# A hybrid encoder layer on one core: bias kept in DRAM in final form, and one DMA per tile for bias, q, k and v

## The chip, the core and the metric

The kernel runs on one core of a Trainium2 chip. The time is that of the device, in microseconds, the median of several executions. A core has five engines that matter here: TensorE (PE in the profile; its weight loads are listed apart as PEld), VectorE (DVE), ScalarE (ACT), GpSimd (POOL) and SyncE (SP), which issues all DMAs of this kernel. A DMA is carried out by up to 16 DMA engines, and SP issues its DMAs in a fixed order: when the next one has to wait for a tile, all that are behind it wait too.

## What is computed

One layer over 512 positions of width 2048, all in float32:

```
h = x @ w_in                                  # 512 x 8192: q, k, v, gate for group A and group B
ya = dilated attention, 16 heads of 64        # logits q.k / 8 + T5 bias by distance, masked to strides 1, 4, 16
yb = neighbourhood attention, 16 heads of 64  # 8 x 64 grid, window 8 x 16, learned bias by (row, column) distance
y = concat(ya * silu(gate_a), yb * silu(gate_b))
x = LayerNorm(2 ** 0.25 * x + y @ w_out)
```

Both attentions are done as dense softmaxes: the bias of a head holds, for 128 queries (8 grid rows x 16 columns) and all keys that can be reached, the bias minus a mask. The kernel subtracts a bias of the opposite sign and takes a minimum in place of a maximum.

## The kernel before

**Stages.** First the input projection in six blocks (`BLOCKS`: v of group A, v of group B, k A, q A, k B, q B), each of 1024 columns. `plain_block` does the first one directly and the others go through `strassen_block`, which does seven products of quarter size. Every float32 operand is split into a high and a low half (`split`, L82 on ScalarE and L83 on VectorE), and each product of tiles is three matmuls. Results are staged in two SBUF buffers (`vst`, tags t4 and t5) and stored to DRAM: v to `v_d[g]` (512 x 2048) by L187, k and q to `kq_d[kind, g]` (8 pairs x 128 x 2 x 512) by L202 and L205.

**Bias before attention.** After block 2 `prep_a` makes one row of 1024 biases per head of group A and writes it 16 times to `rows_d` (L142). After block 3 `prep_b` loads the learned biases of group B, subtracts them from a column mask (L158, L161) and writes 3 variants of 720 values per head and column to `gd` (L162), eight heads at a time. It uses one buffer for its source (tag b0) and one for its result `gt` (tag b1).

**Attention.** 32 heads in 16 pairs; four score tiles per head, so n runs from 0 to 127 (`scores(n)`, head n // 4). PE's order is written out by hand: the scores of tile n, the transposes of tile n - 3 (`turn`), the values of the head before (`values`), and between them `fill(...)`, which takes the next matmuls from a stream of other work: first the gates (16 `gate_unit`s, two weight tiles of 512 KB each), then the first half of the output projection (`out_first`, four column blocks of four weight tiles). What is issued on the other engines and on SP is ordered by the scheduler of the language, from its own estimate of times.

**Loads in attention.** `load_pair(i)` fills the tiles of pair i (tags t0 to t3 for even pairs, t4 to t7 for odd ones): two k tiles, one q tile, one v tile, of 128 x 1024 float32, 512 KB each. A k tile holds the same 64 rows twice, in partitions 0 to 63 and 64 to 127, by two DMAs (L411); q takes four DMAs of 64 partitions (L413), v four of 128 (L418). `load_bias(h)` fills one of two bias buffers (b0, b1) by eight DMAs of 16 partitions each: 560 values per partition out of `rows_d` for group A (L449), 3 x 384 out of `gd` for group B (L452). VectorE reads the bias in L430. Weight tiles for the gates and for `out_first` go through two raw buffers, `raw_ring` (r8, r9), by L110. `out_first` issues four loads of z (the residual x, L546) ahead of its weights.

After attention the second half of the output projection and the normalisation follow (L597 on). They are not touched.

Of the kernel before, what the change touches and what calls it, by code (L numbers as in the profile page):

```python
# [18 lines left out]
PADB = 16  # L19
RPBW = 16 * RPB + 2 * PADB  # L20
# [3 lines left out]
ROW = 1024  # L24
# [34 lines left out]
def _view(t, offset, dims):  # L59
    return bass.AP(tensor=t.tensor, offset=t.offset + offset, ap=dims)  # L60
# [5 lines left out]
def hybrid_layer(tc, xT, xn, w_in, w_gate, w_out, t5x, brow, rpb, cmask, eye, gain, lbias, out):  # L66
    nc = tc.nc
    from contextlib import ExitStack
    with ExitStack() as ctx:
# [3 lines left out]
        dram = ctx.enter_context(tc.tile_pool(name="dram", bufs=1, space=bass.MemoryType.DRAM))  # L73
# [4 lines left out]
        def f(ap):  # L78
            return ap.bitcast(F32)
# [9 lines left out]
        def slot(tag, dtype=F32, name=None):  # L89
            return arena.tile([128, sizes[tag[0]]], dtype, name=name or tag, tag=tag)  # L90
# [32 lines left out]
        nc.vector.memset(eps, EPS)  # L123

        rows_d = dram.tile([H, 16, ROW], F32, name="rows_d")
        gd = dram.tile([H * 16, 3, 720], F32, name="gd")
        kq_d = {(kind, g): dram.tile([PAIRS, 128, 2, S], F32, name=f"{kind}{g}_d") for kind in "kq" for g in range(2)}
        v_d = [dram.tile([S, D], F32, name=f"v{g}_d") for g in range(2)]

        def prep_a():  # L130
            nc.sync.dma_start(ident, eye)
            bt = ring_b.next("bias")
            t5 = bt[0:33, 1024:1040]
            nc.sync.dma_start(bt[0:33, :ROW], brow)
            nc.sync.dma_start(t5, t5x)
            row = ring_b.next("bias")
            for i in range(2):
                ps = bank(pss, "sc")
                nc.tensor.matmul(ps[0:16], t5, bt[0:33, 512 * i:512 * i + 512], start=True, stop=True)
                nc.scalar.activation(row[0:16, 512 * i:512 * i + 512], ps[0:16], AF.Copy)  # L140
            for c in range(16):
                nc.sync.dma_start(rows_d[:, c], row[0:16, :ROW])  # L142

        def prep_b():
            for g in range(2):
                b0 = slot("b0", F32, "rpbs")
                r = b0[:, :720].rearrange("p (d j) -> p d j", d=15)
                masks = b0[:, 720:864].rearrange("p (v j) -> p v j", v=3)
                nc.sync.dma_start(masks, cmask)
                for hh in range(8):  # L150
                    h = 8 * g + hh
                    nc.sync.dma_start(r[16 * hh:16 * hh + 16],
                                      _view(rpb, PADB + h * RPB - 1, [[RPBW - 1, 16], [31, 15], [1, 48]]))
                for v in range(3):
                    gt = slot("b1", F32, "gt")[:, :720].rearrange("p (d j) -> p d j", d=15)
                    w = 32 if v == 0 else 48
                    o = 16 if v == 0 else 0
                    nc.vector.tensor_tensor(gt[:, :, 0:w], masks[:, v:v + 1, 0:w].to_broadcast([128, 15, w]),  # L158
                                            r[:, :, o:o + w], ALU.subtract)
                    if w < 48:  # L160
                        nc.vector.tensor_copy(gt[:, :, w:], masks[:, v:v + 1, w:].to_broadcast([128, 15, 48 - w]))  # L161
                    nc.sync.dma_start(gd[128 * g:128 * g + 128, v], gt)  # L162


        X = [slot(f"x{k}", F32R, f"xk{k}").rearrange("p (s q) -> p s q", s=2) for k in range(KT)]
# [15 lines left out]
        def store_v(g, ch, T, src):  # L181

            o = vst.next("vst", F32R).rearrange("p (h e) -> p h e", h=8)
            s = src.rearrange("p (h e) -> p h e", h=8)
            nc.scalar.activation(o[:, :, 0:64], s, AF.Copy)
            nc.vector.tensor_tensor(o[:, :, 64:128], s, f(o[:, :, 0:64]), ALU.subtract)
            nc.sync.dma_start(v_d[g][128 * T:128 * T + 128, 1024 * ch:1024 * ch + 1024], f(o.rearrange("p h e -> p (h e)")))  # L187

        def store_kq(kind, g, ch, half, b, src):

# [179 lines left out]
        for i, (kind, g) in enumerate(BLOCKS[1:], 1):  # L370
            strassen_block(w_in[16 * i:16 * i + 16], kind, g)
            if i == 2:
                prep_a()
            if i == 3:
                prep_b()

        back = slot("s0", F32, "xback").rearrange("p (k q) -> p k q", k=8)
        for k in range(8):
# [4 lines left out]
        raw_ring, sg_ring = Ring("r8", "r9"), Ring(*(f"n{i}" for i in range(6, 12)))  # L383
# [17 lines left out]
        def load_pair(i):  # L401

            g, j = divmod(i, PAIRS)
            t0 = 4 * (i % 2)
            ks, qs = [], []
            qt = slot(f"t{t0 + 3}", F32R, "q").rearrange("p (a n) -> p a n", a=2)
            for a in range(2):
                kt = slot(f"t{t0 + a}", F32R, f"k{a}").rearrange("p (s n) -> p s n", s=2)
                rows = slice(64 * a, 64 * a + 64)
                for d in range(2):  # L410
                    nc.sync.dma_start(f(kt[64 * d:64 * d + 64]), kq_d["k", g][j][rows])  # L411
                for s in range(2):
                    nc.sync.dma_start(f(qt[64 * s:64 * s + 64, a]), kq_d["q", g][j][rows, s])  # L413
                ks.append(kt)
                qs.append(qt[:, a].rearrange("p (b n) -> p b n", b=4))
            vv = slot(f"t{t0 + 2}", F32R, "vv").rearrange("p (b e) -> p b e", b=4)
            for b in range(4):
                nc.sync.dma_start(f(vv[:, b]), _view(v_d[g], 16 * b * D + 256 * j, [[64 * D, 8], [D, 16], [1, 256]]))  # L418
            return qs, ks, vv.rearrange("p b (h e) -> p b h e", h=2)

        def softmax(sc, bias, n, grp, by_act):
# [22 lines left out]
        def load_bias(h):  # L444
            bias = ring_b.next("bias")
            hg = h % 16
            for r in range(8):
                if h < 16:
                    nc.sync.dma_start(bias[16 * r:16 * r + 16, :560],  # L449
                                      _view(rows_d, hg * 16 * ROW + 463 - 64 * r, [[ROW - 1, 16], [1, 560]]))  # L450
                else:
                    nc.sync.dma_start(bias[16 * r:16 * r + 16].rearrange("p (v n) -> p v n", v=3),  # L452
                                      gd[16 * hg:16 * hg + 16, :, 48 * (7 - r):48 * (7 - r) + 384])
            biases[h] = bias

        def scores(n):
# [82 lines left out]
        def out_first(dc):  # L539

            if dc % 2 == 0:
                for t in range(4):
                    z[t].append(slot(f"x{6 + 2 * t + dc // 2}", F32, f"z{t}").rearrange("p (s q) -> p s q", s=2))
            accs = [bank(pacc, "acc") for _ in range(4)]
            for t in range(4):
                nc.sync.dma_start(z[t][dc // 2][:, dc % 2], xn[t * 128:t * 128 + 128, dc * 512:dc * 512 + 512])  # L546
            for u in range(4):
                wh, wl = out_load(raw_ring, dc, u)
                for t in range(4):
                    yield from out_mms(accs[t], t, u, wh, wl, u == 0, u == 3)  # L550
            for t in range(4):
                zt = z[t][dc // 2][:, dc % 2]
                nc.vector.scalar_tensor_tensor(zt, zt, ALPHA, accs[t], op0=ALU.mult, op1=ALU.add)

        def fillers():
            for _ in range(16):
                yield from gate_unit()
            z.extend([] for _ in range(4))
            for dc in range(4):
                yield from out_first(dc)  # L560
# [77 lines left out]
        for dc in range(2):  # L638
# [4 lines left out]
            for u in range(4, 8):  # L643
                wh, wl = out_load(out_ring, dc, u)
# [81 lines left out]
```

## Time and profile before

| | us |
|---|---|
| median of 3 runs | 1018.22 (1016.59 to 1019.3) |
| the profiled execution | 1024.81 |
| its span, from first to last instruction | 1022.7 |
| TensorE busy in it | 993.1 |
| VectorE busy in it | 752.7 |

The profile is that of one execution, 6.6 us above the median; its span leaves out 2.1 us around it. An engine's busy time counts its instructions; TensorE's matmuls are pipelined, so a busy TensorE is not one at its peak. "DMA share" is the mean busy share of the 16 DMA engines, from the records of their packets; a packet is put down to the stretch in which it starts, so a full stretch can show a little over 1. In the table of stretches each row has the length of the stretch, the busy time and the number of instructions of PE, PEld, DVE, ACT and POOL, the granted clock of TensorE, the DMA share and the GB/s. In the chain of waits each row has start, length and what ran or was waited for. In the timeline and in the list of issues "SPq" is SP's queue; a row's second number is the time that SP took to issue.

### The profile page before, as it was taken

What the parts mean: (1) busy time and instruction counts of PE and PEld (TensorE: products, weight loads), DVE (VectorE), ACT (ScalarE), POOL (GpSimd) and SP (SyncE); (2) the same over time, 40 slices, a digit from 0 to 9 for tenths busy, and PEclk for the clock granted to TensorE, in tenths of its full rate; (3) what the DMA queues carried; (4) which work ended last, traced back from release to release, by engine and by line L of the source; (5) the groups of instructions that cost most, each with busy time, mean ns of one, the idle gap of its engine ahead of it and who ended that gap; (6) DMA issues with size and microseconds to landing.
All of it is one profiled execution on the core that took longest, in us unless ns stands there. A gap on an engine that the chain in (4) does not pass through costs nothing.

```text
span 1022.7 us, 15990 instructions
## 1 busy us (share of the span) xinstructions
PE 993.1 (97%) x5901; PEld 875.0 (86%) x5901; DVE 752.7 (74%) x1257; ACT 517.8 (51%) x862; POOL 13.3 (1%) x13
## 2 busy tenths in 40 slices
PE   9999999999999999999999999999999788999995
PEld 6888888999999999999878888888888677888884
DVE  7826988887887977978577777777766555666677
ACT  6524445444444434445377777777666444656300
POOL 0000000000000000000000000000000000000022
PEclk9999999999999999999999999999999899999998
DMA  9933357347769438347965565566688886745212
GB/s 336 313 99 124 124 156 242 98 135 246 156 195 255 116 115 277 115 125 189 224 186 146 167 167 146 167 167 157 194 224 191 252 206 181 202 144 185 64 62 103
DMA packets 114645, 177.77 MB, mean 174 GB/s; under 512 B 49383, under 2 KB 73575, under 8 KB 114568
## 3 DMA queue, kind: packets, MB, share of 16 engines
q1 hardware_dynamic: 114568, 176.76, 59.1%
q8 instruction: 46, 0.75, 0.3%
q14 instruction: 31, 0.25, 0.1%
HBM read 144.09 MB, written 32.62 MB: 173 GB/s over the span
## 4 chain that ended last, share of the span: by engine, by line
PE 87%; DMA 5%; DVE 4%; SPq 2%; issue 1%; ACT 1%; ACTq 0%; DVEq 0%
PE acc L393 16%; PE acc L535 13%; PE acc L322 9%; PE acc L320 9%; PE acc L321 9%; PE pv L504 4%; PE pt L484 4%; PE acc L315 2%; PE acc L314 2%; PE acc L313 2%; DMA z<-in_xn 2%; PE acc L226 1%; PE acc L225 1%; PE sc L464 1%; PE sc L463 1%; PE acc L224 1%
## 5 line engine op out<-in xcount | busy, mean ns | idle before, releaser
L82 ACT ACTIVATE wh<-braw 128x1024 fp32r<-128x1024 f32 x140 | 148.1, 1060 | 191.4 <-PE acc L321 141.6
L83 DVE TENSOR_TENSOR wl<-braw,wh 128x1024 fp32r<-128x1024 f32 x140 | 170.6, 1222 | 51.1 <-ACT wh L82 50.9
L320 PE MATMUL acc<-xk,wh 128*128 128x256 f32 x512 | 143.3, 282 | 0.6 <-ACT wh L82 0.6
L321 PE MATMUL acc<-xk,wh 128*128 128x256 f32 x512 | 143.1, 281 | 0.0
L393 PE MATMUL acc<-xk,wh 128*128 128x512 f32 x512 | 142.6, 402 | 0.0
L322 PE MATMUL acc<-xk,wl 128*128 128x256 f32 x512 | 140.6, 281 | 0.0
L83 DVE TENSOR_TENSOR wl<-wraw,wh 128x1024 fp32r<-128x1024 f32 (+1 forms) x73 | 88.1, 1207 | 61.8 <-ACT wh L82 57.1
L82 ACT ACTIVATE wh<-wraw 128x1024 fp32r<-128x1024 f32 (+1 forms) x73 | 76.2, 1045 | 72.4 <-DMA wraw<-in_w_out 19.3
L432 ACT ACTIVATE p<-s,mn 128x512 f32<-128x512 f32 (+2 forms) x128 | 81.9, 640 | 60.6 <-DVE mn L430 59.4
L535 PE MATMUL acc<-wh,yk 128*128 128x512 f32 x320 | 108.6, 408 | 0.0
L320 PE MATMUL acc<-op,wh 128*128 128x256 f32 x384 | 107.2, 281 | 0.0
L321 PE MATMUL acc<-op,wh 128*128 128x256 f32 x384 | 107.2, 281 | 0.0
L322 PE MATMUL acc<-op,wl 128*128 128x256 f32 x384 | 105.1, 282 | 1.0 <-DVE wl L83 1.0
L393 PEld LDWEIGHTS acc<-xk,wh 128*128 128x128 f32 x512 | 91.2, 188 | 15.5
L320 PEld LDWEIGHTS acc<-xk,wh 128*128 128x128 f32 x512 | 97.3, 190 | 1.7 <-ACT bias L140 0.9
L321 PEld LDWEIGHTS acc<-xk,wh 128*128 128x128 f32 x512 | 97.3, 190 | 0.0
L327 DVE TENSOR_TENSOR braw<-braw 128x1024 f32<-128x1024 f32 x80 | 96.7, 1220 | 0.7
L322 PEld LDWEIGHTS acc<-xk,wl 128*128 128x128 f32 x512 | 95.8, 190 | 0.0
L490 ACT ACTIVATE th<-pt 128x512 fp32r<-128x512 f32 (+2 forms) x128 | 65.4, 511 | 41.4 <-PE pt L484 40.2
L491 DVE TENSOR_TENSOR tl<-pt,th 128x512 fp32r<-128x512 f32 (+2 forms) x128 | 75.0, 586 | 15.3 <-ACT th L490 14.1
L484 PE MATMUL pt<-ident,p 128*128 128x128 f32 x416 | 67.3, 276 | 13.7 <-DVE tl L491 10.5
L484 PEld LDWEIGHTS pt<-ident,p 128*128 128x128 f32 x416 | 53.2, 142 | 30.5 <-issue 9.8
(157 smaller groups left out, 1866.5 us busy)
## 6 DMA issues: line engine op xcount, KB each, us to landing
braw<-in_w_in SPq DMA_DIRECT2D x80, 512.0 KB
wraw<-in_w_gate SPq DMA_DIRECT2D x32, 512.0 KB
k<-k_d SPq DMA_DIRECT2D x64, 256.0 KB
wraw<-in_w_out SPq DMA_DIRECT2D x32, 512.0 KB
bias<-gd SPq DMA_DIRECT2D x128, 72.0 KB
v_d<-vst SPq DMA_DIRECT2D x16, 512.0 KB
k_d<-kst SPq DMA_DIRECT2D x32, 256.0 KB
q_d<-kst SPq DMA_DIRECT2D x64, 128.0 KB
```

What stands on the lines that cost most here:

```text
L82: nc.scalar.activation(hi, raw, AF.Copy)
L83: nc.vector.tensor_tensor(lo, raw, f(hi), ALU.subtract)
L320: nc.tensor.matmul(o, h[:, c], ah, start=k == 0 and n == 0, stop=False)
L321: nc.tensor.matmul(o, h[:, c], al, start=False, stop=False)
L322: nc.tensor.matmul(o, l[:, c], ah, start=False, stop=k == 7 and n == 1)
L327: nc.vector.tensor_tensor(dst[u], dst[u], other[u], ALU.add)
L393: nc.tensor.matmul(acc, w[:, k * 128:k * 128 + 128], X[8 * u + k][:, s], start=u == 0 and n == 0 and k == 0, stop=u == 1 and n == 2 and k ...
L432: nc.scalar.activation(p[:, :n].rearrange("p (b r c) -> p b r c", r=8, c=16), s[:, :n].rearrange(order, r=8, c=16), AF.Exp, bias=mn, scale ...
L484: nc.tensor.transpose(pt[:, k], p[:, k * 128:k * 128 + 128], ident)
L490: nc.scalar.activation(th, pt[:, :nch], AF.Copy)
L491: nc.vector.tensor_tensor(tl, pt[:, :nch], f(th), ALU.subtract)
L535: nc.tensor.matmul(acc, yk[k][:, s, c], w[:, wk], start=first and kk == 0 and n == 0, stop=last and kk == 1 and n == 2)
```

## The change

The bias of every head is written to DRAM in the form in which attention reads it, `bias_d`: 16 heads x 128 x 560 for group A, 16 x 128 x 1152 for group B. `prep_a` builds its part from `rows_d` by eight DMAs from DRAM to DRAM. `prep_b` is called once for each half of the heads, after blocks 3 and 4, and stores each variant by eight DMAs. `load_bias` is then one DMA. `store_v` splits each tile's store in two, so that `v_d` has its rows in the order in which attention wants them, and v is loaded by one DMA; k takes one DMA per tile, whose source is read twice by a step of 0; q takes two DMAs. `out_first` takes its weights through four buffers (r8, r9, x14, x15) and issues each z load behind a weight load.

```diff
@@ hybrid_layer
-        gd = dram.tile([H * 16, 3, 720], F32, name="gd")
+        bias_d = dram.tile([H, 128, 560], F32, name="biasa_d"), dram.tile([H, 128, 1152], F32, name="biasb_d")
@@ prep_a
+            for r in range(8):
+                nc.sync.dma_start(bias_d[0][:, 16 * r:16 * r + 16],
+                                  _view(rows_d, 463 - 64 * r, [[16 * ROW, 16], [ROW - 1, 16], [1, 560]]))
@@ prep_b
-        def prep_b():
-            for g in range(2):
...
+        def prep_b(g):
...
-                    nc.sync.dma_start(gd[128 * g:128 * g + 128, v], gt)
+                gt = gt.rearrange("p d j -> p (d j)")
+                for k in range(8):
+                    nc.sync.dma_start(bias_d[1][8 * g:8 * g + 8, 16 * k:16 * k + 16, 384 * v:384 * v + 384],
+                                      gt[:, 48 * (7 - k):48 * (7 - k) + 384])
@@ store_v
-            nc.sync.dma_start(v_d[g][128 * T:128 * T + 128, 1024 * ch:1024 * ch + 1024], f(o.rearrange("p h e -> p (h e)")))
+            o = o.rearrange("p h e -> p (h e)")
+            for r in range(2):
+                nc.sync.dma_start(_view(v_d[g], 16 * (2 * T + r) * D + 1024 * ch, [[128 * D, 4], [D, 16], [1, 1024]]),
+                                  f(o[64 * r:64 * r + 64]))
@@ hybrid_layer
-            if i == 3:
-                prep_b()
+            elif i in (3, 4):
+                prep_b(i - 3)
@@ load_pair
-            for a in range(2):
-                kt = slot(f"t{t0 + a}", F32R, f"k{a}").rearrange("p (s n) -> p s n", s=2)
-                rows = slice(64 * a, 64 * a + 64)
-                for d in range(2):
-                    nc.sync.dma_start(f(kt[64 * d:64 * d + 64]), kq_d["k", g][j][rows])
-                for s in range(2):
-                    nc.sync.dma_start(f(qt[64 * s:64 * s + 64, a]), kq_d["q", g][j][rows, s])
...
+            at = 128 * 2 * S * j
+            for s in range(2):
+                nc.sync.dma_start(f(qt[64 * s:64 * s + 64]),
+                                  _view(kq_d["q", g], at + S * s, [[2 * S, 64], [128 * S, 2], [1, S]]))
...
+            for a in range(2):
+                kt = slot(f"t{t0 + a}", F32R, f"k{a}")
+                nc.sync.dma_start(f(kt), _view(kq_d["k", g], at + 128 * S * a, [[0, 2], [2 * S, 64], [1, 2 * S]]))
...
-            for b in range(4):
-                nc.sync.dma_start(f(vv[:, b]), _view(v_d[g], 16 * b * D + 256 * j, [[64 * D, 8], [D, 16], [1, 256]]))
+            nc.sync.dma_start(f(vv), _view(v_d[g], 256 * j, [[D, 128], [128 * D, 4], [1, 256]]))
@@ load_bias
-            for r in range(8):
-                if h < 16:
-                    nc.sync.dma_start(bias[16 * r:16 * r + 16, :560],
-                                      _view(rows_d, hg * 16 * ROW + 463 - 64 * r, [[ROW - 1, 16], [1, 560]]))
-                else:
-                    nc.sync.dma_start(bias[16 * r:16 * r + 16].rearrange("p (v n) -> p v n", v=3),
-                                      gd[16 * hg:16 * hg + 16, :, 48 * (7 - r):48 * (7 - r) + 384])
+            n = 560 if h < 16 else 1152
+            nc.sync.dma_start(bias[:, :n], bias_d[h // 16][hg])
@@ out_first
-            for t in range(4):
-                nc.sync.dma_start(z[t][dc // 2][:, dc % 2], xn[t * 128:t * 128 + 128, dc * 512:dc * 512 + 512])
             for u in range(4):
-                wh, wl = out_load(raw_ring, dc, u)
+                wh, wl = out_load(first_ring, dc, u)
+                nc.sync.dma_start(z[u][dc // 2][:, dc % 2], xn[u * 128:u * 128 + 128, dc * 512:dc * 512 + 512])
                 for t in range(4):
                     yield from out_mms(accs[t], t, u, wh, wl, u == 0, u == 3)
...
+        first_ring = Ring("r8", "r9", "x14", "x15")
```

In a view such as `[[0, 2], [2 * S, 64], [1, 2 * S]]` each pair is a step and a count, in elements, the outermost first.

More of the change, by code (lines that the diff above doesn't have):

```diff
@@ L142, in prep_a @@
                 nc.sync.dma_start(rows_d[:, c], row[0:16, :ROW])
-        def prep_b():
-            for g in range(2):
[L146 to L161, printed above, removed]
-                    nc.sync.dma_start(gd[128 * g:128 * g + 128, v], gt)
@@ new lines, in prep_a @@
+            for r in range(8):
+                nc.sync.dma_start(bias_d[0][:, 16 * r:16 * r + 16],
+                                  _view(rows_d, 463 - 64 * r, [[16 * ROW, 16], [ROW - 1, 16], [1, 560]]))
+        def prep_b(g):
+            b0 = slot("b0", F32, "rpbs")
+            r = b0[:, :720].rearrange("p (d j) -> p d j", d=15)
+            masks = b0[:, 720:864].rearrange("p (v j) -> p v j", v=3)
+            nc.sync.dma_start(masks, cmask)
+            for hh in range(8):
+                h = 8 * g + hh
+                nc.sync.dma_start(r[16 * hh:16 * hh + 16],
+                                  _view(rpb, PADB + h * RPB - 1, [[RPBW - 1, 16], [31, 15], [1, 48]]))
+            for v in range(3):
+                gt = slot("b1", F32, "gt")[:, :720].rearrange("p (d j) -> p d j", d=15)
+                w = 32 if v == 0 else 48
+                o = 16 if v == 0 else 0
+                nc.vector.tensor_tensor(gt[:, :, 0:w], masks[:, v:v + 1, 0:w].to_broadcast([128, 15, w]),
+                                        r[:, :, o:o + w], ALU.subtract)
+                if w < 48:
+                    nc.vector.tensor_copy(gt[:, :, w:], masks[:, v:v + 1, w:].to_broadcast([128, 15, 48 - w]))
+                gt = gt.rearrange("p d j -> p (d j)")
+                for k in range(8):
+                    nc.sync.dma_start(bias_d[1][8 * g:8 * g + 8, 16 * k:16 * k + 16, 384 * v:384 * v + 384],
+                                      gt[:, 48 * (7 - k):48 * (7 - k) + 384])
@@ L404, in load_pair @@
             t0 = 4 * (i % 2)
-            ks, qs = [], []
             qt = slot(f"t{t0 + 3}", F32R, "q").rearrange("p (a n) -> p a n", a=2)
-            for a in range(2):
-                kt = slot(f"t{t0 + a}", F32R, f"k{a}").rearrange("p (s n) -> p s n", s=2)
-                rows = slice(64 * a, 64 * a + 64)
-                for d in range(2):
-                    nc.sync.dma_start(f(kt[64 * d:64 * d + 64]), kq_d["k", g][j][rows])
-                for s in range(2):
-                    nc.sync.dma_start(f(qt[64 * s:64 * s + 64, a]), kq_d["q", g][j][rows, s])
-                ks.append(kt)
-                qs.append(qt[:, a].rearrange("p (b n) -> p b n", b=4))
+            at = 128 * 2 * S * j
+            for s in range(2):
+                nc.sync.dma_start(f(qt[64 * s:64 * s + 64]),
+                                  _view(kq_d["q", g], at + S * s, [[2 * S, 64], [128 * S, 2], [1, S]]))
+            qs = [qt[:, a].rearrange("p (b n) -> p b n", b=4) for a in range(2)]
+            ks = []
+            for a in range(2):
+                kt = slot(f"t{t0 + a}", F32R, f"k{a}")
+                nc.sync.dma_start(f(kt), _view(kq_d["k", g], at + 128 * S * a, [[0, 2], [2 * S, 64], [1, 2 * S]]))
+                ks.append(kt.rearrange("p (s n) -> p s n", s=2))
             vv = slot(f"t{t0 + 2}", F32R, "vv").rearrange("p (b e) -> p b e", b=4)
-            for b in range(4):
-                nc.sync.dma_start(f(vv[:, b]), _view(v_d[g], 16 * b * D + 256 * j, [[64 * D, 8], [D, 16], [1, 256]]))
+            nc.sync.dma_start(f(vv), _view(v_d[g], 256 * j, [[D, 128], [128 * D, 4], [1, 256]]))
             return qs, ks, vv.rearrange("p b (h e) -> p b h e", h=2)
```

## The prediction

> **What bounds the kernel now.** I read the page's first two parts, then the table of stretches, then the chain of waits, then the DMA queue inside the stage that the change touches.
>
> ```profile
> PE 993.1 (97%) x5901; PEld 875.0 (86%) x5901; DVE 752.7 (74%) x1257; ACT 517.8 (51%) x862; POOL 13.3 (1%) x13
> q1 hardware_dynamic: 114568, 176.76, 59.1%
> ```
>
> TensorE is busy 993.1 of 1022.7 us, so all the waits together are worth under 30 us; DMA has two fifths of its time free on average. The table of stretches says where (length, then busy us of PE, PEld, DVE, ACT, POOL, then granted clock, DMA share of the 16 engines, GB/s):
>
> ```profile
> 250.00:330.00 80.00, 79.26 (x661) 77.40 (x660) 65.67 (x71) 34.60 (x39) 0.00 (x0) 1.00 0.73 188
> 330.00:410.00 80.00, 79.71 (x662) 79.31 (x662) 65.80 (x68) 35.33 (x39) 0.00 (x0) 1.00 0.57 176
> 489.00:910.00 421.00, 407.71 (x2060) 340.37 (x2059) 286.00 (x680) 263.42 (x532) 0.00 (x0) 0.98 0.69 185
> 790.00:814.00 24.00, 18.47 (x90) 15.45 (x88) 11.19 (x29) 9.55 (x22) 0.00 (x0) 0.86 0.84 234
> 838.00:862.00 24.00, 19.59 (x84) 16.18 (x85) 13.80 (x38) 10.54 (x24) 0.00 (x0) 0.86 0.72 178
> ```
>
> In attention (489 to 910 us) PE idles 421.00 - 407.71 = 13.3 us, most of it between 790 and 862. The chain of waits names who is late there:
>
> ```profile
> 765.38 5.29 DMA bias<-gd
> 773.28 6.26 DMA z<-in_xn
> 779.56 8.73 DMA z<-in_xn
> 797.52 5.57 DMA z<-in_xn
> 829.89 7.69 DMA k<-k_d
> 840.82 6.05 DMA wraw<-in_w_out
> ```
>
> These are loads queued behind one another. So the kernel is bound by TensorE, with one crowded patch of DMA; the change can win at most those 13.3 us and, at a clock of 0.86 in two stretches of 24 us, about 2 x 24 x 0.14 = 7 us more. It can lose far more if its "large" DMAs turn out to take longer.
>
> **The change part by part. First, the k loads.** Before, each 512 KB k tile is filled by two DMAs of 64 rows of 4 KB. After, it is one DMA whose source is walked as 2 copies (step 0) x 64 rows x 1024 elements. What outermost count does to a DMA can be read from the v load, whose source is walked as 8 x 16 x 256:
>
> ```profile
> 499.97 2.48 SPq L418 DMA_DIRECT2D vv<-v_d  x4
> 502.50 2.40 SPq L411 DMA_DIRECT2D k<-k_d  x4
> 87.10:88.20 1.10, 1.10 (x6) 0.90 (x6) 1.10 (x2) 0.00 (x0) 0.00 (x0) 1.00 0.89 361
> 502.00:504.00 2.00, 2.00 (x10) 1.65 (x10) 0.00 (x0) 0.00 (x0) 0.00 (x0) 1.00 0.48 158
> 506.50:511.00 4.50, 4.50 (x22) 3.72 (x21) 2.67 (x8) 1.53 (x4) 0.00 (x0) 1.00 1.03 229
> 700.10:701.10 1.00, 1.00 (x6) 0.76 (x5) 1.00 (x5) 0.66 (x2) 0.00 (x0) 1.00 0.60 154
> ```
>
> All four v issues are out by 502.45 and k issues follow at once, yet from 502 to 504 the DMA share is 0.48: the v packets keep half of the engines busy and the other half has none. k (outermost count 64, behind them from 506.5) fills all 16 (1.03), and so does the v store (128 partitions, 0.89 with its ends cut off). I read: a DMA is dealt to as many engines as its outermost counts allow, 8 for the v load, and **2 for the new k load**. The trace of before has no DMA with a count of 2, so this step is an inference, and it decides the sign.
>
> The Trainium skill says the same ("DMA: Bandwidth & Descriptors", section "Why a DMA increments its semaphore by 16 and not by 1"): a DMA uses the largest number of engines up to 16 that divides the slowest count of both access patterns. By that rule the v load gets 8, with which 0.48 agrees; no run here yet shows a count of 2.
>
> Price of one engine: the v store moves 361 / (0.89 x 16) = 25.4 GB/s per engine, 0.161 us for a 4 KB row. The new k DMA has 128 rows, 64 per engine: 64 x 0.161 = 10.3 us. 16 pairs x 2 tiles x 10.3 = **330 us on two engines**. Now, 32 tiles of 524 KB (16.8 MB) at 229 / 1.03 = 222 GB/s are 75 us of every engine.
>
> What else those two engines carry in attention: 0.69 x 421 = 290 us, less 75 for k, is 215. The bias loads go from 16 partitions to 128 at a time:
>
> ```profile
> k<-k_d SPq DMA_DIRECT2D x64, 256.0 KB
> bias<-gd SPq DMA_DIRECT2D x128, 72.0 KB
> vv<-v_d SPq DMA_DIRECT2D x64, 128.0 KB
> bias<-rows_d SPq DMA_DIRECT2D x128, 35.0 KB
> ```
>
> 128 x 72 KB + 128 x 35 KB = 14.0 MB, at 154 / 0.60 = 257 GB/s of all engines (the stretch at 700 us, bias alone) is 55 us; at 16 x 25.4 = 406 GB/s it would be 35. So 215 - 20 = 195. v keeps its bytes, on 16 engines instead of 8: twice the engines for half the time, nothing on the sum. q keeps 64 partitions per DMA: nothing.
>
> Sum on the two engines: 330 + 195 = 525 us, where the stage has 421. Free time of an engine now is 0.31 x 421 = 131 us, the k loads add 255: this can't be hidden. **Attention gets 525 - 421 = 104 us longer** if the two engines never idle. They will idle a little, since SP issues in a fixed order and waits at its head for tiles that a stalled PE gives free late; I take 3% of 525, 16 us. Bounds: if k is dealt to 16 engines, 16.8 MB at 406 GB/s is 41 us, 34 less than now; if every wait for bias adds on top (third rival), 90 us more.
>
> **Who waits, and for whom.** All DMAs stand in one queue per engine, so a load dealt to 16 engines lands when the two loaded engines get to it. k is issued early enough for one such delay, bias hardly:
>
> ```profile
> 577.43 3.75 SPq L449 DMA_DIRECT2D bias<-rows_d  x8
> 581.22 1.09 SPq L411 DMA_DIRECT2D k<-k_d  x2
> 588.98 1.08 SPq L411 DMA_DIRECT2D k<-k_d  x2
> 594.27 4.30 SPq L449 DMA_DIRECT2D bias<-rows_d  x6
> 593.78 0.69 DVE L430 CUSTOM_DVE_ANT_0 s<-sc,bias 128x512 f32<-128x512 f32 x1
> ```
>
> The bias issued from 577.43 is first read at 593.78, a lead of 16.3 us; the next one stands behind two k tiles (20.6 us). VectorE would wait in L430, with the low halves of the weights (L83) and of the probabilities (L491) behind it on its queue, and TensorE for those.
>
> **Bias laid out in DRAM (prep_a, prep_b).** New: 8 DRAM-to-DRAM DMAs of 16 heads x 16 rows x 2240 B (4.6 MB, outermost 16: all engines), and 48 stores of 197 KB (9.4 MB) for 6 of 360 KB (2.2 MB). The stores' target is walked as 8 heads x 16 rows: 8 engines by the reading above, 16 rows each; at 25.4 GB/s per engine 9.4 MB take 46 us, 23 per group. The first: nearest row 257 GB/s, 18 us for one pass, twice that if reading and writing add. The free share from 250 to 330 is 0.27 x 80 = 22 us, against 18 + 23 less 5 for the stores removed = 36; from 330 to 410 it is 34 us for 23. About 14 us too much in the first block; the weight tiles' lead covers a part. Also each `gt` waits until eight stores have read its only buffer, 8 us instead of about 1, and on VectorE the weights' low halves stand behind it. I take **+10 us**, between -1 (all hidden) and +30 (every excess and each of the four waits in full). The extra SP time (48 + 8 - 6 issues) is hidden: SP isn't on the chain before 765.
>
> **v stores.** Each tile's store becomes two of 64 partitions, outermost count 4:
>
> ```profile
> 85.98 22.63 SPq L187 DMA_DIRECT2D v_d<-vst  x8
> ```
>
> Now the eight stores of the first block are issued over 22.6 us, 2.8 apart. On 4 engines each takes 16 x 0.161 = 2.6 us, 5.2 per tile; two staging buffers give no more. The fourth to sixth tiles hold accumulator banks that the second product needs. The sixth is late by about 5 x (5.2 - 2.8) = 12 us, against some 8 us until its bank is wanted: **+4 us**, between 0 and +12. The second v block's stores lie far apart: nothing.
>
> **Output projection's first half.** Four raw buffers instead of two, and z loads one at a time between weights. That takes away the three z waits of the chain and 6.05 us of weights, if the queue is free; x14 and x15 come free only when the last gate has read X. In my forecast the two loaded engines are late there anyway: nothing. Fewer issues (28 to 7 per pair, 0.3 to 0.6 us each) are worth only the SPq steps in that patch: nothing, same reason.
>
> **Sum.** 104 + 16 + 10 + 4 = +134 us. The profiled execution took 1024.81 us (span 1022.7 and 2.1 around it); the median of the runs is 1018.22, 6.6 below. 1018 + 134 = 1152; I say 1150.
>
> **Rivals.**
> - *The k load is dealt to 16 engines after all* (split by its 128 partitions). Then attention's DMA falls by 34 for k and 20 for bias, from 0.69 to 0.56, and the queue between 765 and 862 goes: -13 for the idle time, up to -7 for the clock, +4 to +10 for the preparation: 1002 to 1015. For it: nothing but that the v load's half share has one example. It decides at 1018: faster if k has over about 8 engines (41 to 82 us of them). The Trainium skill has advice on this side too ("DMA: Bandwidth & Descriptors", section "Rules for kernel authors": coalesce small transfers; one 128-partition transfer rather than two halves), but the same table warns that an outermost zero-stride broadcast of c copies confines a DMA to c engines. No run here shows either yet.
> - *Two engines, but partly hidden.* k tiles lead by 1.5 pairs, and q and weights may be cheaper on uncrowded engines (215 falls to 160): 330 + 140 - 421 = +49, with 10 for the rest: 1060 to 1085.
> - *The bias waits come on top.* Both k tiles of a pair (20.6 us, some 24 with q and weights) stand ahead of a bias whose lead is 16.3 us: 8 us a pair, and half that again where PE then frees k tiles late and the two engines idle: 15 pairs x 6 to 8 = 90 to 120 more: 1230 to 1260.
> - *The change doesn't touch the bound*: waits of both signs cancel, 1015 to 1021. Only with k on about 8 engines.
>
> **Chances.** Forecast (1085 to 1215) 0.65; partly hidden 0.09; bias on top 0.13; 16 engines 0.10; no change 0.03. Faster by over 0.3% 0.10, within 0.3% 0.03, slower 0.87 (0.3% is about what a measurement of this kernel can tell from no change). The range that leaves out the last two cases and the end of the third: 1060 to 1245.
>
> **What would show it.** Right: stretches in attention with a DMA share near 0.13 at some 50 GB/s, PE idle for over 80 us between 489 and 1030, the chain led by k and bias loads; half shares during `prep_b`'s stores, quarter shares at 86 to 125. Wrong: k loads at a share near 1 and shorter attention. The largest doubt is the step from count 8 to count 2.

## The result, and the profile after

The median went from 1017.89 us (four runs now; the table above has the first three) to 1186.62 us: a ratio of 1.1653 with a 95% interval of 1.1623 to 1.1683, 168.7 us where 132 were forecast. The profiled execution took 1186.8 us, its span is 1185.0. The page after, its first parts and the shares of the chain, and behind them the shares of the chain before:

```profile
PE 1043.0 (88%) x5901; PEld 903.5 (76%) x5901; DVE 751.5 (63%) x1257; ACT 514.7 (43%) x862; POOL 13.3 (1%) x13
q1 hardware_dynamic: 112872, 188.55, 51.9%
PE 46%; DMA 39%; DVE 6%; SPq 3%; ACT 3%; issue 2%; DVEq 0%; POOL 0%; ACTq 0%; POOLq 0%
```

```profile
PE 87%; DMA 5%; DVE 4%; SPq 2%; issue 1%; ACT 1%; ACTq 0%; DVEq 0%
```

The engines do the same work (VectorE 751.5 us against 752.7), the DMA engines are on average less busy than before (51.9% against 59.1%), and yet DMA is now 39% of the chain that sets the end, where it was 5%. A mean over 16 engines hides what two of them do. The stages say where the time is. Here and below a block's stretch begins with its first matmul and ends with its last one or with the next block's first, and attention goes from the first gate matmul to the last score tile; first the five stretches after, then the same five before:

```profile
92.90:197.10 104.20, 84.83 (x337) 66.17 (x336) 66.14 (x68) 37.72 (x44) 0.00 (x0) 0.92 0.39 134
197.30:282.80 85.50, 83.08 (x678) 81.05 (x676) 69.76 (x72) 36.83 (x41) 0.00 (x0) 1.00 0.48 164
282.80:375.80 93.00, 84.64 (x673) 83.82 (x673) 64.92 (x68) 34.41 (x38) 0.00 (x0) 0.94 0.80 223
375.80:464.20 88.40, 83.08 (x674) 82.67 (x674) 68.05 (x71) 35.03 (x38) 0.00 (x0) 0.96 0.77 240
544.10:1096.80 552.70, 460.30 (x2138) 374.41 (x2137) 299.72 (x718) 273.10 (x558) 0.00 (x0) 0.91 0.50 147
```

```profile
93.90:169.90 76.00, 76.00 (x337) 62.92 (x337) 65.98 (x68) 36.45 (x41) 0.00 (x0) 1.00 0.54 180
170.10:252.60 82.50, 82.50 (x677) 80.88 (x675) 67.67 (x70) 37.01 (x41) 0.00 (x0) 1.00 0.46 154
252.60:332.80 80.20, 79.46 (x674) 79.22 (x674) 65.58 (x70) 34.16 (x38) 0.00 (x0) 1.00 0.76 199
332.80:414.20 81.40, 81.11 (x674) 80.70 (x673) 67.42 (x69) 35.06 (x38) 0.00 (x0) 1.00 0.56 174
494.10:934.50 440.40, 427.11 (x2140) 355.94 (x2138) 301.50 (x718) 275.97 (x558) 0.00 (x0) 0.98 0.67 183
```

The rows are the block v B, the blocks k A, q A and k B, and attention. They grew by 28.2, 3.0, 12.8, 7.0 and 112.3 us, together 163.3; the span grew by 162.3, so the rest is as long as before. TensorE's 460.30 busy us in attention against 427.11 are the same matmuls at a granted clock of 0.91 for 0.98 (427.11 x 0.98 / 0.91 = 460). In these rows the clock is lowest where TensorE idles most: 0.92 with 19 of 104 us idle in the block v B, 0.91 with 92 of 553 in attention, 1.00 with none.

Two stretches of the table of the changed kernel in which little but one kind of DMA runs, and what the chain waits for in the block v B and in attention:

```profile
88.60:99.60 11.00, 7.16 (x32) 5.60 (x30) 0.69 (x1) 0.60 (x1) 0.00 (x0) 0.94 0.26 93
593.00:595.00 2.00, 0.13 (x1) 0.13 (x2) 2.00 (x3) 1.82 (x4) 0.00 (x0) 1.00 0.13 53
```

```profile
88.42 11.47 DMA v_d<-vst
101.90 8.95 DMA v_d<-vst
112.82 9.40 DMA v_d<-vst
...
166.98 11.65 DMA v_d<-vst
180.67 11.67 DMA v_d<-vst
194.38 12.91 DMA v_d<-vst
...
587.87 18.04 DMA bias<-biasa_d
615.35 19.82 DMA bias<-biasa_d
635.18 17.95 DMA wraw<-in_w_gate
...
897.61 25.04 DMA k<-k_d
```

The v stores, whose target has an outermost count of 4, run at a share of 0.26, a quarter of the engines. The k loads run at 0.13, two of sixteen, at 53 GB/s, 26.5 per engine. That is the step that the forecast had to infer. What the chain then names is mostly not k (2% of it): it is bias (16%) and weights (10%), which by the same reading are dealt to all engines and wait 18 to 20 us until the two loaded ones reach them. Whoever reads the names alone would blame the bias.

### The profile page after: what moved, and what is told of

Same layout as the page of the kernel before. It is cut to its first block, busy times and chain, and to the rows that moved or that the text cites. A ratio compares the mean times of both kernels' runs of the same rounds, so it can differ in the third digit from the quotient of the medians.

```text
span 1185.0 us, 15632 instructions
## 1 busy us (share of the span) xinstructions
PE 1043.0 (88%) x5901; PEld 903.5 (76%) x5901; DVE 751.5 (63%) x1257; ACT 514.7 (43%) x862; POOL 13.3 (1%) x13
## 3 DMA queue, kind: packets, MB, share of 16 engines
q1 hardware_dynamic: 112872, 188.55, 51.9%
## 4 chain that ended last, share of the span: by engine, by line
PE 46%; DMA 39%; DVE 6%; SPq 3%; ACT 3%; issue 2%; DVEq 0%; POOL 0%; ACTq 0%; POOLq 0%
DMA bias<-biasb_d 10%; PE acc L537 8%; DMA wraw<-in_w_gate 7%; DMA bias<-biasa_d 6%; PE acc L330 6%; PE acc L328 6%; PE acc L329 6%; DMA v_d<-vst 6%; PE acc L401 4%; DMA wraw<-in_w_out 3%; DMA k<-k_d 2%; DVE wl L83 2%; SPq L166 2%; DMA biasb_d<-gt 2%; ACT wh L82 2%
## 5 line engine op out<-in xcount | busy, mean ns | idle before, releaser
L401 PE MATMUL acc<-xk,wh 128*128 128x512 f32 x512 | 158.6, 438 | 1.7 <-ACT wh L82 1.7
L486 PE MATMUL pt<-ident,p 128*128 128x128 f32 x416 | 72.7, 292 | 59.5 <-DVE tl L493 52.3
L330 PE MATMUL acc<-op,wl 128*128 128x256 f32 x384 | 108.4, 291 | 13.1 <-DVE wl L83 13.0
L401 PEld LDWEIGHTS acc<-xk,wh 128*128 128x128 f32 x512 | 101.9, 211 | 20.5 <-ACT wh L82 2.1
L328 PE MATMUL acc<-op,wh 128*128 128x256 f32 x384 | 109.8, 288 | 2.4 <-ACT wh L82 2.4
L329 PE MATMUL acc<-op,wh 128*128 128x256 f32 x384 | 109.5, 288 | 0.0
L328 PEld LDWEIGHTS acc<-xk,wh 128*128 128x128 f32 x512 | 97.6, 191 | 2.4 <-ACT wh L82 1.5
L329 PEld LDWEIGHTS acc<-xk,wh 128*128 128x128 f32 x512 | 97.5, 191 | 0.0
L437 DVE CUSTOM_DVE_ANT_0 s<-sc,bias 128x512 f32<-128x512 f32 (+1 forms) x96 | 61.3, 638 | 38.0 <-DMA bias<-biasa_d 25.1
```

Of the source, the lines that this page charges most:

```text
L328: nc.tensor.matmul(o, h[:, c], ah, start=k == 0 and n == 0, stop=False)
L329: nc.tensor.matmul(o, h[:, c], al, start=False, stop=False)
L330: nc.tensor.matmul(o, l[:, c], ah, start=False, stop=k == 7 and n == 1)
L401: nc.tensor.matmul(acc, w[:, k * 128:k * 128 + 128], X[8 * u + k][:, s], start=u == 0 and n == 0 and k == 0, stop=u == 1 and n == 2 and k ...
L437: nc.vector.tensor_tensor_reduce(*flat, bias, 1.0, 3e38, ALU.add, ALU.min, mn)
L486: nc.tensor.transpose(pt[:, k], p[:, k * 128:k * 128 + 128], ident)
```

## The experiments

Lengths are in us: the block v B; the blocks k A, q A and k B together; attention; then the median, the ratio to the kernel before on the same chip and its 95% interval. The medians of the kernel before there were 1022.61 (first four runs), 1017.95 (next four) and 1021.33 (last four).

| kernel | v B | three blocks | attention | median | ratio |
|---|---|---|---|---|---|
| before | 75.9 | 244.1 | 440.3 | 1017.89 | |
| changed | 104.2 | 266.9 | 552.7 | 1186.62 | 1.1653 (1.1623 to 1.1683) |
| k_two_dmas | 100.2 | 265.4 | 422.5 | 1053.79 | 1.0309 (1.0285 to 1.0333) |
| k_one_dma_alone | 75.9 | 244.5 | 634.5 | 1219.32 | 1.1929 (1.1901 to 1.1956) |
| v_store_undone | 75.9 | 265.1 | 562.8 | 1166.38 | 1.1406 (1.1388 to 1.1425) |
| bias_undone | 102.7 | 247.4 | 599.4 | 1212.24 | 1.1840 (1.1798 to 1.1882) |
| k_copies_128rows | 100.9 | 297.1 | 422.5 | 1099.68 | 1.0798 (1.0763 to 1.0834) |
| k_copies_2x64 | 103.7 | 297.3 | 555.3 | 1236.28 | 1.2130 (1.2088 to 1.2171) |
| k_count4 | 104.0 | 269.9 | 448.6 | 1084.39 | 1.0638 (1.0598 to 1.0679) |
| all_three_undone | 75.9 | 243.7 | 431.2 | 1015.93 | 0.9976 (0.9956 to 0.9996) |
| bias_new_only | 75.9 | 264.8 | 427.0 | 1030.71 | 1.0097 (1.0064 to 1.0129) |
| bias_A_only | 75.9 | 249.9 | 430.1 | 1020.82 | 1.0003 (0.9985 to 1.0021) |
| bias_b_by_rows | 75.9 | 249.9 | 439.8 | 1030.32 | 1.0097 (1.0059 to 1.0136) |
| v_store_by_16 | 77.1 | 243.9 | 430.8 | 1014.50 | 0.9933 (0.9915 to 0.9951) |

### The k load undone

```diff
-                nc.sync.dma_start(f(kt), _view(kq_d["k", g], at + 128 * S * a, [[0, 2], [2 * S, 64], [1, 2 * S]]))
+                for d in range(2):
+                    nc.sync.dma_start(f(kt[64 * d:64 * d + 64]),
+                                      _view(kq_d["k", g], at + 128 * S * a, [[2 * S, 64], [1, 2 * S]]))
```

> The changed kernel, with each k tile loaded by two DMAs of 64 rows again; all else as changed. Theory (a DMA is dealt to as many engines as its outermost counts allow, and the k load with a count of 2 costs the attention stage 112 us): from the first gate matmul to the last score tile, 440.3 us before and 552.7 after, comes back to 425 to 445, and the median to 1060 to 1078. Rival (the stage is late because bias and weights each come in one DMA, in another order on SP's queue): the stage stays above 500 and the median above 1135.

Attention falls from 552.7 to 422.5, more than expected, and is 18 us shorter than in the profile before the change. The stretch of this kernel and its issues of bias:

```profile
538.80:961.30 422.50, 421.71 (x2140) 352.37 (x2138) 299.99 (x717) 276.02 (x558) 0.00 (x0) 1.00 0.68 190
L457 SPq DMA_DIRECT2D bias<-biasa_d x16: 326/530/821, 425.5 to 723.1; - x16
L457 SPq DMA_DIRECT2D bias<-biasb_d x16: 326/536/617, 735.7 to 930.9; - x16
```

TensorE is busy 421.71 of 422.50 us at full clock: it hardly waits any more. All of the change's loss in attention is the k load, 130 us. The other edits win up to 18 there (440.3 to 422.5); part of that is the profiled execution of the kernel before, which stood 6.6 us above its median. The rival about bias and SP's order falls.

### The k load alone

```diff
-                for d in range(2):
-                    nc.sync.dma_start(f(kt[64 * d:64 * d + 64]), kq_d["k", g][j][rows])
+                nc.sync.dma_start(f(kt.rearrange("p s n -> p (s n)")),
+                                  _view(kq_d["k", g], 128 * 2 * S * j + 128 * S * a, [[0, 2], [2 * S, 64], [1, 2 * S]]))
```

> The kernel before, with only the k load changed (one DMA per tile, source walked as 2 x 64 x 1024). Theory: two engines carry 330 us of k rows beside some 215 us of the rest; the stage grows by 100 to 125 us, the projection not at all; median 1115 to 1140. Rival (the loss needs the other edits too, a late one-piece bias above all): median below 1065.

A miss on the high side: attention is 194 us longer, not 100 to 125, and the kernel is worse than the whole change. The loss doesn't need the other edits; on the contrary, they make it 82 us smaller (634.5 against 552.7). Undoing one of them in the changed kernel shows the same. Here the chain does name the k loads first, with 21.6% of the span against 2% in the changed kernel: whom it names depends on what else stands in the queue.

### The v store undone, and the bias undone

The v store is as before, and with it the load by four DMAs:

```diff
-            for r in range(2):
-                nc.sync.dma_start(_view(v_d[g], 16 * (2 * T + r) * D + 1024 * ch, [[128 * D, 4], [D, 16], [1, 1024]]),
-                                  f(o[64 * r:64 * r + 64]))
+            nc.sync.dma_start(v_d[g][128 * T:128 * T + 128, 1024 * ch:1024 * ch + 1024], f(o.rearrange("p h e -> p (h e)")))
```

> The changed kernel, with v stored by one DMA of 128 partitions per tile and loaded by four DMAs, as before. Theory (stores with an outermost count of 4 run on 4 engines and hold up the second v block): that block, 75.9 us before and 104.2 after, comes back to 75 to 78, median 1156 to 1162. Rival (the v block's delay is only a start-up effect that later waits would have cost anyway): median above 1175.

The block v B is back at 75.9; with it the block k A, which began behind the last stores, lost its 3 us (82.5). The median came down less than expected, since attention grew by 10, where v is loaded by four DMAs again.

For the bias, `prep_a`, `prep_b` and `load_bias` are those of the kernel before, and the call of `prep_b` with them.

> The changed kernel, with the bias of both groups prepared and loaded as before (rows_d, gd, eight DMAs per head). Theory (the preparation costs the three blocks from k A to k B 22 us in all; in attention the late bias only stands behind k): those blocks come back to 242 to 248 us together, the attention stage stays at 530 to 565, median 1150 to 1175. Rival (bias in one DMA is itself what attention waits for): the stage falls below 500 and the median below 1125.

The blocks came back (247.4), but attention got 47 us longer, to 599.4; neither theory had that. What SP needs to issue a bias load (minimum, median and maximum in ns), first in the changed kernel, then with the bias undone, then in the kernel before:

```profile
L455 SPq DMA_DIRECT2D bias<-biasa_d x16: 326/1046/6139, 430.3 to 785.2; - x16
L455 SPq DMA_DIRECT2D bias<-biasb_d x16: 321/1533/8664, 802.6 to 1066.5; - x16
```

```profile
L451 SPq DMA_DIRECT2D bias<-rows_d x128: 302/418/7368, 329.1 to 794.3; - x128
L454 SPq DMA_DIRECT2D bias<-gd x128: 537/591/10690, 799.8 to 1106.2; - x128
```

```profile
L449 SPq DMA_DIRECT2D bias<-rows_d x128: 302/418/1805, 299.5 to 683.1; - x128
L452 SPq DMA_DIRECT2D bias<-gd x128: 537/591/1400, 692.4 to 909.0; - x128
```

With two engines loaded, one issue can hold SP for 6 to 11 us, and all that is behind it; without, none takes over 0.82 in k_two_dmas (above) and none over 1.8 in the kernel before. So with a confined DMA in the queue the number of issues has a price that it doesn't have otherwise. That this is the whole of the 47 us wasn't tested, but the rest of the engines' work hardly grew. The stage of this run, and of the k load alone:

```profile
524.20:1123.60 599.40, 469.07 (x2138) 378.77 (x2138) 297.51 (x717) 273.10 (x558) 0.00 (x0) 0.89 0.47 136
493.10:1127.60 634.50, 474.96 (x2139) 383.84 (x2138) 300.19 (x718) 273.03 (x558) 0.00 (x0) 0.86 0.43 129
```

A share of 0.47 over 599.4 us is 282 us per engine in the mean, against 0.50 x 552.7 = 276 in the changed kernel.

### Is it the count, the step of 0, or the size of the DMA?

Both kernels store k twice (four stores of 64 partitions where there was one of 128, which costs the three blocks 30 us in both) and load a tile by one DMA of 512 KB; they differ in how the copies lie.

```diff
-                nc.sync.dma_start(f(kt), _view(kq_d["k", g], at + 128 * S * a, [[0, 2], [2 * S, 64], [1, 2 * S]]))
+                nc.sync.dma_start(f(kt), _view(kd2[g], at * 2 + 256 * S * a, [[2 * S, 128], [1, 2 * S]]))              # 128rows
+                nc.sync.dma_start(f(kt), _view(kd2[g], at * 2 + 128 * S * a, [[256 * S, 2], [2 * S, 64], [1, 2 * S]]))  # 2x64
```

> The changed kernel, with k stored twice in DRAM (8.4 MB more stores) so that the 128 rows of a tile follow one another; a tile is still one DMA of 512 KB. Theory (the count of 2 is what confines it): k runs on 16 engines and on all partitions; the attention stage (first gate matmul to last score tile, 552.7 in the changed kernel) falls to 410 to 430. Rival (one DMA per tile is the fault, by its size): the stage stays above 520.

> As the run with 128 rows in a row, but with the two copies of a tile's rows apart in DRAM: the load's source is 2 x 64 x 1024 with a step that isn't 0. Theory (the count decides, not the step of 0): two engines again, the stage at 535 to 570 and over 110 us longer than with 128 rows in a row. Rival (reading the same rows twice is what is slow): the stage at 410 to 440.

The stretch of attention, first with 128 rows in a row, then with 2 x 64:

```profile
586.60:1009.10 422.50, 421.45 (x2139) 352.51 (x2138) 301.52 (x718) 276.62 (x558) 0.00 (x0) 1.00 0.60 190
```

```profile
590.80:1146.10 555.30, 461.23 (x2138) 374.23 (x2137) 299.67 (x718) 273.33 (x558) 0.00 (x0) 0.91 0.50 147
```

422.5 against 555.3, with the same bytes, the same number of DMAs and the same stores: the outermost count of 2 is the cause, with a step of 0 or without. One large DMA per tile is harmless, and with all 128 partitions in it the share is 0.60 where two of 64 make 0.68.

A count of 4 in between: two DMAs per tile again, the rows in DRAM in groups of 16 with gaps.

```diff
+                                      _view(kg[g], at * 2 + 256 * S * a, [[64 * S, 4], [2 * S, 16], [1, 2 * S]]))
```

> The changed kernel, with each k tile in two DMAs of 64 rows, whose rows stand in DRAM in groups of 16 with gaps, so that the source is 4 x 16 x 1024 (the k stores get a count of 8 with it). Theory (the busiest engines' sum against the stage's length): k takes 165 us on four engines, with some 220 of other work 385, less than the 422 that the stage takes without the fault: the stage at 420 to 445, nearly no loss. Rival (the loss is proportional to the slowness of the DMA): a loss of 130 x (1/4 - 1/16) / (1/2 - 1/16) = 56 us, the stage at 470 to 490.

448.6: 26 us of loss, 4 above the theory's range and far under the rival's. The stage of this run:

```profile
546.00:994.60 448.60, 429.60 (x2139) 357.00 (x2138) 300.79 (x718) 276.13 (x558) 0.00 (x0) 0.98 0.67 180
```

The theory's 385 us for the four engines was too low. By this row an engine is busy 0.67 x 448.6 = 301 us in the mean; the 165 us of k on four engines are 41 of them, so the rest is 260 and the four engines have 425 (an estimate from this row, with the rest dealt evenly). That is the length of the stage without the fault, 422. What the 26 us are made of isn't shown.

### What the rest is worth

> The changed kernel with k in two DMAs, v stored and loaded as before, and the bias prepared and loaded as before. What is left of the change is q in two DMAs, four weight buffers in the first half of the output projection, and z loads between the weights. Theory (these hit the crowded patch of the stage, 13 us idle and 7 us of clock): the stage at 425 to 436, the projection as before, the time 4 to 15 us under the kernel before. Rival (the gain of the stage without the k fault, 18 us, is the bias' alone): within 3 us of the kernel before.

The stage is at 431.2, 9 us under before, as expected, and the profiled span 10 us under (1012.3 against 1022.7), but the median is only 2.0 us lower, 0.24%: under what the theory gave, and inside the rival's 3 us. The profile of the kernel before is that of an execution 6.6 us above its median, and little of this can lie outside attention: there, in all_three_undone and in v_store_by_16 (below), the stage begins at 494.1, 492.8 and 494.2 us, and 88.2, 88.3 and 88.3 us follow it. So most of these 9 us aren't the edits'. The rest of the 18 us:

> The changed kernel with k in two DMAs and v stored and loaded as before: the new bias in both groups, q in two DMAs, and the rings stay. Theory (the bias in one DMA is what shortens the attention stage from 431.2 to 422.5, and its preparation costs 20 us in the three blocks from k A to k B, 244.1 before): the stage at 421 to 426, the blocks at 261 to 268, the time 5 us over to 5 us either side of that, 1018 to 1028. Rival (v in one DMA shortens the stage): the stage at 429 to 433, the time 1030 to 1038.

427.0 in the stage, neither the theory's 421 to 426 nor the rival's 429 to 433. By the profiles the bias gives 4.2 us (from 431.2), and the v load in one DMA the 4.5 from there to 422.5 (k_two_dmas). These are differences of single executions on different chips, where executions of one kernel differ by 2 to 9 us, so the split isn't shown. The medians give the bias more: this kernel is 9.4 us over the kernel before with 20.7 us of preparation, so some 11 us come back, where all_three_undone wins 2.0. The preparation costs 20.7 us (264.8 against 244.1), and the kernel is 1% behind the one before.

> As bias_new_only, with group B's bias prepared and loaded as before. Theory (the preparation's cost is mostly the 48 stores of group B): the three blocks at 246 to 254, the stage at 426 to 432, since group B's loads crowd it; the time 1013 to 1022. Rival (the eight DMAs from DRAM to DRAM are what delays the blocks): the blocks above 258.

The blocks grow by 5.8 us (249.9) with the eight DMAs from DRAM to DRAM, so the 48 stores of group B have the other 15. The time is that of the kernel before.

```diff
-                    nc.sync.dma_start(bias_d[1][8 * g:8 * g + 8, 16 * k:16 * k + 16, 384 * v:384 * v + 384],
+                    nc.sync.dma_start(bias_d[1][k, 128 * g:128 * g + 128, 384 * v:384 * v + 384],
...
+                nc.sync.dma_start(bias[:, :n], _view(bias_d[1], 16 * hg * 1152, [[H * 16 * 1152, 8], [1152, 16], [1, 1152]]))
```

> As bias_new_only, with group B's bias in DRAM as 8 x 256 x 1152, so that a store's target is 128 rows at one step (count 128, 16 engines) and a load's source is 8 x 16 x 1152 (count 8). Theory (the stores' count of 8 doubles their time, and the wait for the one buffer with it): the three blocks fall by 6 to 12 us against bias_new_only, the stage stays within 4 us. Rival (it is the bytes and the number of stores): the blocks within 3 us of bias_new_only.

With a count of 128 for 8 in the same 48 stores, the blocks fall by 14.9 us, more than the 6 to 12 expected, to those of bias_A_only: the stores cost nothing that can be seen. But the count of 8 now stands in the load, and the stage, expected within 4, grew by 12.8 (427.0 to 439.8). The time is the same. The cost was moved, not removed.

### A version that beats the kernel before

k and bias as before (k in two DMAs), q, the weight buffers and z as changed, v loaded by one DMA, and each v tile stored by eight DMAs of 16 partitions. Against the changed kernel:

```diff
-            for r in range(2):
-                nc.sync.dma_start(_view(v_d[g], 16 * (2 * T + r) * D + 1024 * ch, [[128 * D, 4], [D, 16], [1, 1024]]),
-                                  f(o[64 * r:64 * r + 64]))
+            for r in range(2):
+                for b in range(4):
+                    nc.sync.dma_start(v_d[g][128 * b + 16 * (2 * T + r):128 * b + 16 * (2 * T + r) + 16, 1024 * ch:1024 * ch + 1024],
+                                      f(o[64 * r + 16 * b:64 * r + 16 * b + 16]))
```

> The kernel with only k and the bias undone, and each v tile stored by eight DMAs of 16 partitions (count 16) in place of two of 64 (count 4); v is loaded by one DMA. Theory (the count is what made the v stores hold up the second block): that block at 76 to 80 where two stores of 64 give 100 to 104; the attention stage at 427 to 431; the time 1010 to 1018. Rival (reading 16 partitions at a time is as slow as four engines): the block at 90 or more.

The stretches of the block v B and of attention in this kernel:

```profile
93.00:170.10 77.10, 76.57 (x336) 62.72 (x335) 66.60 (x69) 37.11 (x43) 0.00 (x0) 1.00 0.61 153
494.20:925.00 430.80, 424.79 (x2139) 354.58 (x2138) 301.31 (x718) 276.91 (x558) 0.00 (x0) 0.99 0.70 187
```

The block is at 77.1 where two stores of 64 partitions gave 104.2, so the count was the fault there too. The time is 0.67% under the kernel before (0.9933, 0.9915 to 0.9951), the lowest ratio of all that were measured. Against all_three_undone it wasn't measured side by side. Their ratios to the kernel before, each on its own chip, have intervals that don't meet (0.9956 to 0.9996 there), which speaks for a gain by the v load in one DMA, but their own medians lie only 1.4 us apart.

## Why the prediction was right, and where it was off

- **k load on two engines, 10.3 us a tile, 330 us in all**: right. The share of 0.13 at 53 GB/s gives 16.8 MB / 53 = 317 us; the pair of runs with copies shows that the count does it. The Trainium skill's table ("DMA: Bandwidth & Descriptors", section "Rules for kernel authors") names the zero-stride broadcast as an example of an outermost count under 16; these runs agree that the count decides, since with another step the stage is no better, 555.3 us.
- **What else the two engines carry, 195 us, and 16 us of idling**: 541 in all, where the stage took 552.7. Right as a sum, with some luck in the terms. In the changed kernel an engine is busy 0.50 x 552.7 = 276 us in the mean; k's 317 us on two engines are 40 of that, so the rest is 237, not 195, and 317 + 237 = 554 fills the stage without any idling (an estimate, if the rest is dealt evenly). The rest was 42 too small; k was 13 and the idling 16 too large. As a growth it was +120 against +112, and against a median execution of the kernel before the measured growth would be some us larger.
- **The same working with the k load alone** gives 330 + 215 + 16 = 561, and the stage took 634.5. Two things can be missing there, and their shares weren't measured: v loads at a count of 8 put their time on half of the engines, and SP is held by its issues. The term for v, "twice the engines for half the time, nothing on the sum", holds for the mean of 16 engines and not for two of them; v_store_undone puts it, with three more issues a pair, at 10 us (562.8 against 552.7). The Trainium skill ("DMA: Bandwidth & Descriptors", section "Why a DMA increments its semaphore by 16 and not by 1") says that the lowest-numbered engines are taken; by that the two loaded engines are among the eight. No view of these traces shows which engines ran.
- **Bias in front of attention, +10 with a range to +30**: measured 20 us (the blocks q A and k B grew by 19.8). The mechanism was right, eight engines and a wait for the one `gt` buffer, which the chain now names three times, with the DMAs from DRAM to DRAM ahead of it; the size was too low by half. Of the 20.7 us in bias_new_only, 15 go with the count of 8 and 6 with the DRAM-to-DRAM part.

```profile
301.32 10.85 DMA biasa_d<-rows_d
326.96 6.01 DMA biasb_d<-gt
339.75 6.30 DMA biasb_d<-gt
415.19 6.37 DMA biasb_d<-gt
```

- **v stores, +4, the second block nothing: this step failed.** Measured 28 us in the block v B and 3 in the block after it. Most of it comes from the first block's stores, which are still under way when the block v B begins. The same matmuls of this block in three parts, after and then before:

```profile
92.90:134.10 41.20, 28.24 (x98) 20.41 (x97) 26.12 (x26) 13.49 (x18) 0.00 (x0) 0.83 0.28 102
134.10:172.20 38.10, 38.10 (x170) 31.55 (x169) 28.13 (x30) 14.96 (x15) 0.00 (x0) 1.00 0.41 126
172.20:197.30 25.10, 18.69 (x74) 14.38 (x73) 12.09 (x13) 9.32 (x12) 0.00 (x0) 0.93 0.56 199
```

```profile
93.90:115.70 21.80, 21.80 (x98) 18.03 (x97) 21.54 (x22) 11.98 (x15) 0.00 (x0) 1.00 0.24 97
115.70:153.80 38.10, 38.10 (x170) 31.56 (x169) 31.57 (x34) 16.52 (x18) 0.00 (x0) 1.00 0.52 164
153.80:170.10 16.30, 16.30 (x74) 13.50 (x72) 13.07 (x14) 7.98 (x10) 0.00 (x0) 1.00 0.97 326
```

  The first part, beside the first block's stores (waits of 11.47, 8.95 and 9.40 us in the chain), is 19.4 us longer, where +4 with a range to +12 was forecast. The last part, beside the second block's own stores, is 8.8 us longer, and 3 more follow in the next block. The forecast took these stores for far apart. The chain shows them in pairs of tiles: four stores of 256 KB, 2.8 us each at 93 GB/s, stand before two staging buffers, the next pair waits 11.65, 11.67 and 12.91 us for them, and ScalarE waits in order with the weights' high halves behind it.
- **Fewer issues, four weight buffers, z between weights: nothing.** Not so. While k is confined, the edits of attention other than k are worth 82 us (634.5 against 552.7); undoing the bias alone costs 47 of that, though the engines' mean work hardly grows, so the number of issues most likely counts there, which the forecast put at nothing. With k on 16 engines they are worth up to 18 us in the profiles, and less in the medians.
- **Rivals.** Sixteen engines: out. Bias waits on top (1230 to 1260): out for this kernel, but k_one_dma_alone is close to it with 1219. Partly hidden, no change: out.

The sum was +134 and the result +169. Of the 35 missing, 27 are the v stores and 10 the bias, with 8 too many in attention; the other 6 are no part of the change: the profiled execution of the kernel before stood 6.6 us above its median, that of the changed one didn't. As most of these lie in attention, the 8 too many there are in part the same 6.

## What to carry to other kernels

Before merging DMAs look at the outermost count of both sides. Here loads and stores with counts of 16, 64 and 128 did no harm, while a broadcast by a leading step of 0, a reordered store and a per-head layout left 2, 4 and 8 engines, and the mean DMA share fell while the kernel waited. Add up the time of the busiest engines and set it against the stage's length: with a sum of about that length (k_count4, some 425 against 422) the loss was 26 us, with one far over it (554) 130 us. Everything else in the queue is then late, and the chain can name loads that aren't at fault. Look at both ends of a layout: a count taken out of the store can come back in the load.

## What was not expected of the hardware

A DMA on few engines also holds up the engine that issues. In the changed kernel SP took up to 8.7 us for one bias load and a median of 1.5 us in group B; with k on 16 engines (k_two_dmas) the same loads took at most 0.62. With eight loads per head and two loaded engines one issue took up to 10.7 us. And reading 16 partitions at a time cost the v stores next to nothing, 77.1 us for the block against 75.9.
